# A hybrid conv and attention encoder layer on eight cores: attention moved one group further behind the projections, and the conv work regrouped

## The chip, the cores and the metric

The kernel runs on all 8 cores of one Trainium2 chip. Each core takes half of one prompt sequence (4,096 frames) and four sample streams, and no core waits for another. Times are device microseconds (us) of the slowest core. A ratio is the mean time of one kernel's fast runs over that of the other kernel's fast runs of the same rounds, so it is not quite the ratio of the medians that stand beside it.

Some executions fall in a slower state, in which one die or both show a lower granted TensorE clock. A variant is compared by its ratio to the kernel before on its own chip. For finer statements the cores of a die that the slow state left alone are used as well: in each run the slowest core of the less disturbed die, called the undisturbed die below. By that measure the kernel before takes 2670 to 2673 us (medians) on four chips. On the first chip it cannot be formed for the kernel before, whose runs there are on record without core clocks; its profiled run took 2678.91 us where the four timed runs took about 2700.

## The reference, cut to what matters

One encoder layer, applied to every frame:

```python
x = x + 0.5 * swiglu_ffn(x, g_ff1, w_ff1_in, w_ff1_out)            # first pass
z = rms_norm(x, g_mix) @ w_in                                      # the mixer starts here
cv, cg, q, k, v = jnp.split(z, SPLITS, axis=-1)
u = cv * jax.nn.sigmoid(cg)                                        # GLU, 512 channels
c_out = silu(layer_norm(depthwise_conv31(u_hist) + b_dw))
q = partial_rope(rms_norm(q, g_q), pos)                            # 8 heads of 64
k = partial_rope(rms_norm(k, g_k), pos)                            # 2 heads of 64
a_out = banded_window_attention(q, k, v, sinks)                    # own chunk of 64 and two before
x = x + jnp.concatenate([c_out, a_out], axis=-1) @ w_out           # the mixer ends here
x = x + 0.5 * swiglu_ffn(x, g_ff2, w_ff2_in, w_ff2_out)            # third pass
```

## The kernel before

The program has three passes: the first feed-forward pass (names that begin with A_), the mixer (B_) and the second feed-forward pass, here called the third pass (C_). The mixer handles 32 groups of 128 frames; eight groups make a conv tile. The Python code writes the operations in program order. From it come the dependencies. A list scheduler then assigns every operation a place in its engine's instruction stream, using assumed durations. Where an operation wasn't ready when its turn came, TensorE was seen to stand before it, for 3.27 us in the first timeline below. The names to know:

- B_xn, B_wi: projections (GLU, q, k, v). B_um: the GLU's result.
- B_qn: normed, rotated q and k. TensorE transposes it and VectorE copies the transpose to B_qkt, which the scores read.
- B_pt: the exponentials of the scores, B_ma: the attention result.
- B_us, B_wr: the conv's input and weights, B_y its output, B_yb a bf16 copy for the sums of the layer norm, B_lr the reciprocal deviation, B_z the conv's result.
- B_z goes through memory in another layout and comes back through the staging buffer B_mt into B_mc. The output projection multiplies B_mc and B_ma by B_wo and adds B_x.
- C_wu: weights of the third pass in 22 column groups. C_xb: its first normed blocks.

One step of the mixer, before:

```python
proj, att = n < NG, 1 <= n <= NG               # NG = 32 groups
...
if proj:
    self.glu_pe(n); self.glu_act(n)            # GLU projection, sigmoid
if att:
    self.transp(trq, 128, self.QKT[n % 4])     # transpose the q and k of the previous step
...
if cq is not None:
    self.conv_pe(cq[0], cq[1], 0)              # one pair of 32-channel conv groups a step, from step 10
    self.conv_pe(cq[0], cq[1], 1)
if att:
    self.scores(n - 1, 0)                      # scores that read the transpose made in this step
...
if att:
    self.scores(n - 1, 1)
tail_some(2)
if proj:
    self.qkv_pe(...)                           # q, k, v of group n
if att:
    self.pv(n - 1)
if proj:
    trq, f = self.qkv_post(n, ...)             # norm and rotation of q and k: ScalarE and VectorE
...                                            # from step 22: output projection of group n - 22
```

The conv of the first tile uses two accumulator banks, one of which the attention also uses:

```python
if t == 0:
    p = self.pb[6 if half == 0 else 4][:, 0:N]     # scores and pv use banks 4 and 5
else:
    p = self.pb[6][:, half * 256:half * 256 + 256]
```

Of the kernel before, what the change touches and what calls it, by code (L numbers as in the profile page):

```python
# [22 lines left out]
class _Op:  # L23
    __slots__ = ("eng", "fn", "idx", "lane", "seq", "deps", "raw", "waits", "know", "signal", "tok", "cost", "nbytes", "unit")


class Prog:
# [124 lines left out]
    def schedule(self, rounds=3):  # L152
# [15 lines left out]
        dma = [l[0].lane is not None for l in units]  # L168
        wire = [l[0].nbytes / 250e3 if d else 0.0 for l, d in zip(units, dma)]

# [55 lines left out]
        for i in range(rounds):  # L226
            start, order, t = run(preds, succs, prio, False)
            if best is None or t < best[0]:
                best = (t, order)
            start, _, _ = run(succs, preds, [-(start[u] + cost[u]) for u in range(n)], True)  # L230
            prio = [-(start[u] + cost[u]) for u in range(n)]
            self.trace.append(t)
        self.order = [o for u in best[1] for o in units[u]]
        self.model_us = best[0]

    def resolve(self):
# [97 lines left out]
class Ops:  # L334
# [4 lines left out]

    def cost(self, eng, meth, kw):  # L340
        out = kw.get("out", kw.get("ap"))
        n = free_size(kw["in_"] if meth == "tensor_reduce" else out)
        if eng == "tensor":
            if meth == "transpose":
                return 0.11 if kw["in_"].dtype == BF16 else 0.25
            return max(0.105, n / 2400.0 + 0.003)
        if eng == "scalar":
            ptr = sum(hasattr(kw.get(k), "tensor") for k in ("scale", "bias"))
            return 0.28 + 0.093 * max(0, ptr - 1) + n / 1200.0 + (0.2 if kw.get("accum_out") is not None else 0)
        if eng == "gpsimd":  # L350
            return 0.2 + n * 0.0022
        aps = [kw[k] for k in OUTS + INS if hasattr(kw.get(k), "tensor")]
        psum = any(self.P.info[a.tensor.name][0] == "p" for a in aps)
        one = meth in ("tensor_copy", "tensor_scalar")
        fast = 2.0 if one and not psum else 1.0
        if all(a.dtype == BF16 for a in aps) and meth in ("tensor_copy", "tensor_scalar", "tensor_tensor"):
            fast *= 2.0
        return 0.14 + n / 960.0 / min(fast, 4.0)

# [82 lines left out]
class FF:  # L442
# [3 lines left out]
    def __init__(self, K, carves, tag, wu, wd, g1, g2, blocks, src, dst, xnd=None, rkey=None, wkey=None, nkey=None, low=None, cwd=None, weng="gpsimd", hook=None):  # L446
# [14 lines left out]
        fits = NJ if low is None else (low - c1.off) // 4096  # L461
        self.WU = [(c1 if j < fits else c2)([128, 2048], BF16, "wu") for j in range(NJ)]
        c3 = c0 if cwd is None else cwd
# [195 lines left out]
GLAG = 22  # L659
NG = 32  # L660


class Mixer:
# [5 lines left out]
    def __init__(self, K, base):  # L669
# [18 lines left out]
        self.GE = [C([128, 512], F32, "ge") for _ in range(2)]  # L688
        self.UX = C([128, 4, 4, 56], BF16, "ux")
        self.VC = C([128, 4, 128], BF16, "vc")  # L690
        self.KCT = C([128, 4, 128], BF16, "kct")
        self.SMASK = C([64, 256], BF16, "smask")
        self.QKS = C([128, 5, 64], BF16, "qks")
        self.VS = C([64, 128], BF16, "vs")
        self.US32 = C([128, 4, 64], F32, "us32")
        self.U32 = self.US32[:, :, 0:32]
        self.QKT = [C([128, 5, 128], BF16, "qkt") for _ in range(4)]
        self.V = [C([128, 128], BF16, "v") for _ in range(4)]
        self.PT = [C([128, 2, 512], BF16, "pt") for _ in range(3)]
# [3 lines left out]
        self.WO = C([128, 8, 1024], BF16, "wo")  # L703
        self.MA = [C([128, 4, 128], BF16, "ma") for _ in range(GLAG - 1)]
        self.MC = C([128, 4, 1024], BF16, "mc")
# [11 lines left out]

        self.WR = [C([128, 2, 1152], BF16, "wr") for _ in range(2)]
        self.US_off = C.off
# [10 lines left out]
        self.LR = C([128, 304], F32, "lr")  # L730
        se = C.off
        self.SE = C([128, 4, 304], F32, "se")
        self.LT = self.SE[:, 3, :]
        self.OUT = P.sbuf("B_out", [128, 512], F32, se)
        self.Z = C([128, 4, 304], BF16, "z")
        self.ZS = C([128, 4, 16], BF16, "zs")
        self.ZT = C([128, 16, 16], BF16, "zt")
        self.MT = [P.sbuf("B_mt0", [128, 8, 256], BF16, se), P.sbuf("B_mt1", [128, 8, 256], BF16, y)]
        self.end = C.off
# [190 lines left out]
    def scores(self, G, kg):  # L930
        O = self.O
        two = self.two(2) if kg == 0 else self.two(4)
        K_ = self.QKT[(G + kg) % 4]
        Q = self.QKT[(G + 1) % 4]
        with self.O.group():
            for g in range(2):
                r = slice(g * 64, g * 64 + 64)
                O.mm(two[:, g * 512:(g + 1) * 512], K_[r, 4, :], Q[r, 0:4, :])
        pt = self.PT[self.nxt("pt", 3)]
        self.pts[kg] = pt  # L940
        O.act(out=pt[:, :, :].rearrange("p g n -> p (g n)"), in_=two, func=AF.Exp, scale=0.125)
# [4 lines left out]
    def pv(self, G):  # L946
# [3 lines left out]
        for half in range(2):  # L950
            ps = self.pb[4 + half]
            with self.O.group():
                combos = ((half, slice(0, 128)), (1 - half, slice(0, 64) if half == 0 else slice(64, 128)))
                for ci, (kg, rows) in enumerate(combos):
                    for what in range(2):
                        for g in range(2):
                            mv = self.pts[kg][rows, g, :].rearrange("p (j q) -> p j q", j=4)[:, :, half * 64:half * 64 + 64]
                            if what == 0:
                                w = self.V[(G + kg) % 4][rows, g * 64:(g + 1) * 64]
                            else:  # L960
                                w = self.ONE[rows, 1 if (G == 0 and kg == 0) else 0, :]
# [53 lines left out]
    def load_wd(self, q):  # L1015
        i = self.nxt("wr", 2)
        self.wr[q] = self.WR[i]
        self.O.dma("sync", "bwr%d" % i, self.WR[i][:, :, :], self.d.wdc[2 * q:2 * q + 2].rearrange("g p n -> p g n"),
                   rk=[("wdc", g, h) for g in (2 * q, 2 * q + 1) for h in range(2)])

    def conv_pe(self, t, q, half):
# [3 lines left out]
        if t == 0:  # L1025
            p = self.pb[6 if half == 0 else 4][:, 0:N]
        else:
# [4 lines left out]
        self.yps[half] = p  # L1032

    def conv_post(self, t, q):
        O = self.O
        N = 304 if t == 0 else 256
        sl = self.ypos % self.NY
        self.ypos += 2
        yb, y2 = self.YB[q % 2], self.Y2[q % 2]
        for h in range(2):  # L1040
            g = 2 * q + h
            O.act(out=self.Y[:, sl + h, 0:N], in_=self.yps[h], func=AF.Identity, bias=self.CP[:, 0, g:g + 1])
            self.yslot[(t, g)] = sl + h
        ys = self.Y[:, sl:sl + 2, 0:N]
# [126 lines left out]
    def run(self, on_step=None):  # L1171
# [3 lines left out]
        last_step = NG + GLAG  # L1175
        CL = 10

# [13 lines left out]
        def conv_at(n):  # L1191
            c = n - CL
            return divmod(c, 8) if 0 <= c < 32 else None

        trq = None
        for n in range(last_step):
            proj, att = n < NG, 1 <= n <= NG
            cq = conv_at(n)
            og = n - GLAG
            flush_late()  # L1200
            if n == 0:
# [4 lines left out]
                self.transp(QN, 128, self.QKT[0], q=False)  # L1206
            nq = conv_at(n + 1)
            if nq is not None:
                self.load_wd(nq[1])
            if 0 <= og + 1 < NG:  # L1210
# [5 lines left out]
            if proj:  # L1216
                self.glu_pe(n)
                self.glu_act(n)
            if att:
                self.transp(trq, 128, self.QKT[n % 4])  # L1220
            if self.stat:
                q = self.stat.pop()
                self.stats_pe(q[1])
                if q[1] == 7:
                    self.tails.append(self.tail(q[0]))
            if proj:
                self.glu_dve(n)
            if cq is not None:
                self.conv_pe(cq[0], cq[1], 0)
                self.conv_pe(cq[0], cq[1], 1)  # L1230
            if att:
                self.scores(n - 1, 0)
            if cq is not None:
                self.conv_post(cq[0], cq[1])
                self.stat.append((cq[0], cq[1]))
            if att:
                self.scores(n - 1, 1)
            tail_some(2)
# [5 lines left out]
            if att:  # L1244
                self.pv(n - 1)
            if proj:
                lastg = n == NG - 1
                trq, f = self.qkv_post(n, 128, self.two(2), self.V[(n + 1) % 4][:, :], k32=self.KO[:, :] if lastg else None,
                                       v32=self.VO[:, :] if lastg else None)
            if att:  # L1250
                self.late.append(self.softmax_group(n - 1))
            if proj:
                self.late.append(f)
            for h in range(2):
                tt = n - (6 + 2 * h) - (2 if h else 0)
                if tt >= 0 and tt % 8 == 0 and tt // 8 < 4:
                    self.load_us(tt // 8, h)
# [74 lines left out]
def build_nc():  # L1332
# [81 lines left out]
    def prologue():  # L1414
# [8 lines left out]
    c0 = Carve(P, base, "C")  # L1423
    c2 = Carve(P, M.US_off, "C_")
    Cc = FF(K, (c0, c0, c2), "C", d.wu2b, d.wd2b, d.gains[2], None, [main[0:2] + [samp]] + b3, d.x2, d.yout, rkey=lambda g: [("x2", g[0])],
            low=M.mid, weng="sync")
    assert c0.off <= M.US_off
    Cc.run(loads(Cc))
# [113 lines left out]
```

## Time and profile before

| | before |
|---|---|
| median of four runs | 2700.36 us (2697.87 to 2704.14) |
| span of the profiled core | 2677.2 us |
| TensorE busy over the span | 93% |

The mean of 93% hides where the time goes. This is the busy time by stretches of the kernel before, on its slowest core: from the end of the first pass to the first output projection, from there to the last group's projection, from there to the last output projection, and the third pass. Columns: the stretch, its length, then busy time (and number of instructions) of TensorE's matmuls, its weight loads, VectorE, ScalarE and GpSimd, then the granted TensorE clock, the busy share of the DMA engines, and GB/s.

```profile
1055.00:1401.00 346.00, 283.50 (x1817) 143.97 (x1815) 182.97 (x443) 191.36 (x324) 29.55 (x57) 0.88 0.30 78
1401.00:1534.00 133.00, 131.97 (x847) 70.45 (x846) 85.43 (x179) 77.22 (x132) 18.70 (x31) 0.99 0.56 168
1534.00:1740.00 206.00, 149.31 (x830) 79.80 (x828) 114.26 (x294) 75.88 (x112) 38.53 (x67) 0.85 0.70 224
1740.00:2677.00 937.00, 923.06 (x5351) 516.11 (x5349) 243.88 (x598) 162.71 (x304) 18.15 (x34) 0.99 0.17 58
```

Read the first row: TensorE idles for 346.0 - 283.5 = 62.5 us, and what it does it does at a mean clock of 0.88. In the second row it idles for 1 us: there the output projections give it something to do whatever else is late. In the third it idles for 57 us. No other engine is near its limit in the first row (VectorE 183 of 346 us), so it is waiting, not bandwidth, that costs time.

What TensorE waited for in that first stretch. Columns: who waited, for whom, the name of what it waited for, us in total, number of waits, the longest.

```profile
PE PS L363 <- DVE B_qn L363: 26.4, 9, 4.3
PE PS L363 <- DVE B_qkt L363: 8.1, 12, 1.0
PE PS L363 <- DVE B_t_95 L363: 6.0, 3, 2.9
PE PS L363 <- ACT B_y L363: 5.9, 1, 5.9
PE PS L363 <- DVE B_t_94 L363: 2.9, 1, 2.9
```

More than half of it is the chain of one group's q and k: norm on ScalarE and VectorE (B_qn), transpose on TensorE, copy on VectorE (B_qkt), scores on TensorE. The timeline of TensorE in the kernel before shows one such place (start, us, engine, operation, operands, and in brackets the idle time just before and its releaser):

```profile
1270.82 0.27 PE L363 MATMUL PS<-B_y_170,B_e_158 128*128 128x256 bf16 x1
1274.37 0.44 PE L363 MATMUL PS<-K_t,B_qn 128*128 128x128 bf16 x5 [3.27 <-DVE B_qn L363]
1275.08 2.44 PE L363 MATMUL PS<-B_us,B_wr 128*128 128x304 bf16 x9 [0.27 <-DVE B_ma L363]
```

TensorE stands for 3.27 us before the five transposes (B_qn). The nine conv matmuls after the gap take 2.44 us; the same nine take 1.33 us elsewhere in this trace. The granted clock over those 2.44 us was 0.50. The gap is paid twice, once as idle time and once as slow matmuls. The slow ones need not be the first: after the gap of 2.93 us that ends at 1287.26 us the nine took 1.35 us, and the next nine, at 1290.86, took 2.46 us.

After the last projection, TensorE of the kernel before waited for:

```profile
PE PS L363 <- DVE C_xb L363: 19.8, 2, 10.6
PE PS L363 <- DVE B_mc_164 L363: 9.9, 2, 5.9
PE PS L363 <- DMA B_wr<-wdc: 6.4, 1, 6.4
PE PS L363 <- DMA C_wu<-wu2b: 5.0, 1, 5.0
```

### The profile page before, as it was taken

Reading aid. Unit: us, or ns where it says so; the run is one execution under the profiler, and the core shown is the slowest. Engines: PE = TensorE matmul, PEld = TensorE weight load, DVE = VectorE, ACT = ScalarE, POOL = GpSimd, SP = SyncE. Lnnn points to the kernel's source line nnn. Section 1 sums busy time; section 2 is a strip of 40 time slices with the busy share of each in tenths; the row PEclk is TensorE's granted clock in tenths of the full one; section 3 lists DMA queues with packets and bytes.
Section 4 is the critical chain, followed back from the end, with each engine's and each line's share of the span. In section 5 each row is a group of like instructions: output and inputs, shape, how many; then the busy total and the mean of one; then the engine's idle time right before and its main releaser. Section 6 shows DMA issues by size and latency. Waiting matters only on the chain.

```text
span 2677.2 us, 41546 instructions; the slowest of 8 cores (2662.2 to 2677.2 us)
## 1 busy us (share of the span) xinstructions
PE 2485.1 (93%) x14740; PEld 1367.4 (51%) x14740; DVE 1030.0 (38%) x2717; ACT 764.4 (29%) x1311; POOL 224.7 (8%) x398
## 2 busy tenths in 40 slices
PE   1999999999999999798869976799999999999998
PEld 1555555555555555344435543355555555555554
DVE  2253344334433424444467556422232333223211
ACT  1222232223222312555466545011111121112110
POOL 2010111011100001000021111200000000000000
PEclk9999999999999999898879988899999999999999
DMA  9943444345433344122235685750121112110110
GB/s 196 173 124 79 87 116 107 80 96 120 119 80 85 87 124 143 36 57 79 71 97 151 207 266 171 228 191 29 48 71 48 42 54 72 56 48 32 48 48 24
DMA packets 113698, 266.93 MB, mean 100 GB/s; under 512 B 33631, under 2 KB 51039, under 8 KB 112535
## 3 DMA queue, kind: packets, MB, share of 16 engines
q0 software_dynamic: 36416, 131.81, 19.5%
q1 hardware_dynamic: 77079, 132.46, 17.2%
q8 instruction: 121, 1.98, 0.3%
q14 instruction: 82, 0.67, 0.1%
HBM read 230.89 MB, written 97.86 MB: 123 GB/s over the span
## 4 chain that ended last, share of the span: by engine, by line
PE 85%; DMA 7%; DVE 4%; issue 2%; ACT 1%; DVEq 0%; POOL 0%; ACTq 0%; POOLq 0%; SPq 0%
PE PS L363 85%; DMA A_wd<-wd 4%; DVE B_y L363 1%; DMA B_wr<-wdc 1%; DMA xnt<-A_xo 0%; DMA A_wu<-wu 0%; DMA B_x_152<-x 0%; DVE B_qs L363 0%; DVE C_sm L363 0%; DMA C_xa<-x 0%; ACT B_sq L363 0%; DVE B_t_94 L363 0%; DVE B_qn L363 0%; ACT B_se L363 0%; DMA x<-B_x_152 0%
## 5 line engine op out<-in xcount | busy, mean ns | idle before, releaser
L363 PE MATMUL PS<-A_xnt,A_wu 128*128 128x384 bf16 (+1 forms) x3872 | 651.0, 329 | 1.8 <-ACT A_xnt L363 1.0
L363 PE MATMUL PS<-C_xnt,C_wu 128*128 128x384 bf16 (+1 forms) x3872 | 628.0, 324 | 6.3 <-DMA C_wu<-wu2b 5.0
L363 PEld LDWEIGHTS PS<-A_xnt,A_wu 128*128 128x128 bf16 x3872 | 377.3, 98 | 258.9 <-issue 6.4
L363 PEld LDWEIGHTS PS<-C_xnt,C_wu 128*128 128x128 bf16 x3872 | 378.4, 98 | 247.1 <-issue 6.9
L363 ACT ACTIVATE C_sa<-PS 128x384 f32<-128x384 f32 (+1 forms) x242 | 117.5, 486 | 757.7 <-PE PS L363 724.7
L363 PE MATMUL PS<-A_wd,A_h 128*128 128x512 bf16 (+1 forms) x1496 | 327.1, 379 | 2.4 <-DMA A_wd<-wd 2.4
L363 PE MATMUL PS<-C_wd,C_h 128*128 128x512 bf16 (+1 forms) x1452 | 315.3, 379 | 0.0
L363 DVE TENSOR_TENSOR C_h<-PS,C_sa 128x384 bf16<-128x384 f32 (+1 forms) x242 | 133.3, 551 | 368.6 <-PE PS L363 362.0
L363 DVE TENSOR_TENSOR A_h<-PS,A_sa 128x384 bf16<-128x384 f32 (+1 forms) x242 | 136.2, 563 | 330.5 <-PE PS L363 329.0
L363 ACT ACTIVATE A_sa<-PS 128x384 f32<-128x384 f32 (+1 forms) x242 | 120.1, 496 | 411.4 <-PE PS L363 376.2
L363 PEld LDWEIGHTS PS<-A_wd,A_h 128*128 128x128 bf16 (+1 forms) x1496 | 146.3, 98 | 175.3 <-issue 3.8
L363 PEld LDWEIGHTS PS<-C_wd,C_h 128*128 128x128 bf16 (+1 forms) x1452 | 142.7, 98 | 169.5 <-issue 0.4
L363 DVE SCALAR_TENSOR_TENSOR C_xr<-PS,C_xr 128x512 f32<-128x512 f32 (+1 forms) x66 | 45.6, 691 | 270.6 <-PE PS L363 270.6
L363 PE MATMUL PS<-B_xn,B_wi 128*128 128x512 bf16 x512 | 123.6, 390 | 2.1 <-ACT B_ge L363 0.9
L363 ACT ACTIVATE A_xb<-A_xr 128x1024 bf16<-128x1024 f32 (+1 forms) x34 | 36.0, 1057 | 285.5 <-DVE A_xr L363 266.8
L363 DVE SCALAR_TENSOR_TENSOR A_xr<-PS,A_xr 128x512 f32<-128x512 f32 (+1 forms) x68 | 46.8, 689 | 160.2 <-PE PS L363 160.2
L363 PE MATMUL PS<-B_us,B_wr 128*128 128x256 bf16 (+1 forms) x576 | 91.6, 315 | 17.3 <-DMA B_wr<-wdc 6.4
L363 PE MATMUL PS<-B_wi,B_xn 128*128 128x256 bf16 (+1 forms) x512 | 94.1, 338 | 0.8 <-ACT B_pt L363 0.8
L407 POOL DMA_DIRECT2D yout<-C_xr x33 | 17.6, 534 | 909.3 <-DVE C_xr L363 909.3
L363 PE MATMUL PS<-K_t,A_xb 128*128 128x128 bf16 (+1 forms) x544 | 42.0, 223 | 53.5 <-DVE A_sm L363 31.3
L363 PEld LDWEIGHTS PS<-B_us,B_wr 128*128 128x128 bf16 x576 | 60.2, 109 | 46.6 <-issue 27.2
L363 PEld LDWEIGHTS PS<-B_xn,B_wi 128*128 128x128 bf16 x512 | 48.5, 100 | 61.8 <-issue 15.1
(169 smaller groups left out, 2033.2 us busy)
## 6 DMA issues: line engine op xcount, KB each, us to landing
B_wr<-wdc SPq DMA_DIRECT2D x32, 576.0 KB, 4.8
A_xa<-xin SPq DMA_DIRECT2D x33, 512.0 KB, 5.4
A_xr<-xin SPq DMA_DIRECT2D x33, 512.0 KB, 3.7
x<-A_xr POOLq DMA_DIRECT2D x33, 512.0 KB, 2.9
C_xa<-x SPq DMA_DIRECT2D x32, 512.0 KB, 3.7
C_xr<-x SPq DMA_DIRECT2D x32, 512.0 KB, 3.7
yout<-C_xr POOLq DMA_DIRECT2D x32, 512.0 KB, 2.9
A_wu<-wu POOLq DMA_DIRECT2D x22, 512.0 KB, 39.0
```

The source lines that it names most:

```text
L363: o = self.P.add(eng, lambda e: getattr(e, meth)(**kw), r, w, cost=self.cost(eng, meth, kw))
L407: self.P.add(eng, lambda e: e.dma_start(out=out, in_=in_), r, w, lane=lane, rk=rk, wk=wk, cost=1.0 if eng == "gpsimd" else 0.5, nbytes=n * ...
```

## The change

The intent: give the chain of one group's q and k a whole step more before its result is needed; do a tile's conv in four steps and leave the next four free of conv, so that its layer norm on VectorE can spread over eight; put the first tile's conv in one bank; load the third pass's weights so that those whose memory comes free last are used last; and correct the scheduler's assumed durations. Its core, with cuts:

```diff
# scheduler: assumed durations (cut)
-        wire = [l[0].nbytes / 250e3 ...]
+        wire = [l[0].nbytes / (210e3 if l[0].eng == "gpsimd" else 290e3) ...]
-        fast = 2.0 if one and not psum else 1.0          # assumed of VectorE: single-source operations twice as fast
+        if meth == "tensor_copy":                        # assumed of copies alone
+            fast = (2.0 if half else 1.0) if psum else (4.0 if half else 2.0)
# buffers
-        self.QKT = [... for _ in range(4)]; self.V = [... for _ in range(4)]
+        self.QKT = [... for _ in range(5)]; self.V = [... for _ in range(5)]
-        self.OUT = P.sbuf("B_out", [128, 512], F32, se)              # shared with the norm's scratch
+        self.OUT = self.GE[0]
-        self.MT = [P.sbuf("B_mt0", [128, 8, 256], BF16, se), ...]    # shared with the norm's scratch
+        self.MT = [C([128, 8, 256], BF16, "mt"), ...]
# mixer step
-            proj, att = n < NG, 1 <= n <= NG
+            proj, tra, att = n < NG, 1 <= n <= NG, 2 <= n <= NG + 1
-                self.scores(n - 1, 0) ... self.scores(n - 1, 1) ... self.pv(n - 1)
+                self.scores(n - 2, 0) ... self.scores(n - 2, 1) ... self.pv(n - 2)
-        CL = 10
-            c = n - CL
-            return divmod(c, 8) if 0 <= c < 32 else None
+        CL = 8
+            t, r = divmod(n - CL, 8)
+            return [(t, 2 * r), (t, 2 * r + 1)] if 0 <= t < 4 and r < 4 else []
-            p = self.pb[6 if half == 0 else 4][:, 0:N]
+            p = self.pb[6][:, 0:N]                 # tile 0: evict the first half before the second
+                self.load_wd((q + 2) % 8)          # conv weights two pairs ahead
# third pass's weights
-        self.WU = [(c1 if j < fits else c2)([128, 2048], BF16, "wu") for j in range(NJ)]
+        self.WU = [c1([128, 2048], BF16, "wu") for j in range(min(fits, NJ))]
+        self.WU += [c2([128, 2048], BF16, "wu") for j in range(fits, NJ)][::-1]
```

More of the change, by code (lines that the diff above doesn't have):

```diff
@@ L23 @@
 class _Op:
-    __slots__ = ("eng", "fn", "idx", "lane", "seq", "deps", "raw", "waits", "know", "signal", "tok", "cost", "nbytes", "unit")
+    __slots__ = ("eng", "fn", "idx", "lane", "seq", "deps", "raw", "waits", "know", "signal", "tok", "cost", "nbytes", "unit", "t")
 class Prog:
@@ L168, in schedule @@
         dma = [l[0].lane is not None for l in units]
-        wire = [l[0].nbytes / 250e3 if d else 0.0 for l, d in zip(units, dma)]
+        wire = [l[0].nbytes / (210e3 if l[0].eng == "gpsimd" else 290e3) if d else 0.0 for l, d in zip(units, dma)]
         def run(before, after, prio, back):
@@ L228, in schedule @@
             if best is None or t < best[0]:
-                best = (t, order)
+                best = (t, order, start)
             start, _, _ = run(succs, preds, [-(start[u] + cost[u]) for u in range(n)], True)
@@ L234, in schedule @@
         self.model_us = best[0]
+        for u, l in enumerate(units):
+            for o in l:
+                o.t = best[2][u]
     def resolve(self):
@@ L344, in cost @@
             if meth == "transpose":
-                return 0.11 if kw["in_"].dtype == BF16 else 0.25
-            return max(0.105, n / 2400.0 + 0.003)
+                return 0.1 if kw["in_"].dtype == BF16 else 0.25
+            w = kw["lhsT"].ap
+            t = n / 2400.0 + 0.005
+            if w[0][1] <= 64 and w[-1][1] > 64:
+                return 0.75 * t
+            if w[-1][1] <= 64:
+                return max(0.06, 0.78 * t)
+            return max(0.101, t)
         if eng == "scalar":
             ptr = sum(hasattr(kw.get(k), "tensor") for k in ("scale", "bias"))
-            return 0.28 + 0.093 * max(0, ptr - 1) + n / 1200.0 + (0.2 if kw.get("accum_out") is not None else 0)
+            return 0.2 + 0.093 * ptr + n / 1200.0 + (0.2 if kw.get("accum_out") is not None else 0)
         if eng == "gpsimd":
@@ L353, in cost @@
         psum = any(self.P.info[a.tensor.name][0] == "p" for a in aps)
-        one = meth in ("tensor_copy", "tensor_scalar")
-        fast = 2.0 if one and not psum else 1.0
-        if all(a.dtype == BF16 for a in aps) and meth in ("tensor_copy", "tensor_scalar", "tensor_tensor"):
-            fast *= 2.0
-        return 0.14 + n / 960.0 / min(fast, 4.0)
+        half = all(a.dtype == BF16 for a in aps)
+        fast = 1.0
+        if meth == "tensor_copy":
+            fast = (2.0 if half else 1.0) if psum else (4.0 if half else 2.0)
+        return 0.15 + n / 960.0 / fast
     def op(self, eng, meth, **kw):
@@ L660 @@
 NG = 32
+NWR = 2
 class Mixer:
@@ L688, in __init__ @@
         self.GE = [C([128, 512], F32, "ge") for _ in range(2)]
-        self.UX = C([128, 4, 4, 56], BF16, "ux")
-        self.VC = C([128, 4, 128], BF16, "vc")
-        self.KCT = C([128, 4, 128], BF16, "kct")
-        self.SMASK = C([64, 256], BF16, "smask")
-        self.QKS = C([128, 5, 64], BF16, "qks")
-        self.VS = C([64, 128], BF16, "vs")
         self.US32 = C([128, 4, 64], F32, "us32")
         self.U32 = self.US32[:, :, 0:32]
-        self.QKT = [C([128, 5, 128], BF16, "qkt") for _ in range(4)]
-        self.V = [C([128, 128], BF16, "v") for _ in range(4)]
+        self.QKT = [C([128, 5, 128], BF16, "qkt") for _ in range(5)]
+        self.V = [C([128, 128], BF16, "v") for _ in range(5)]
         self.PT = [C([128, 2, 512], BF16, "pt") for _ in range(3)]
@@ L703, in __init__ @@
         self.WO = C([128, 8, 1024], BF16, "wo")
-        self.MA = [C([128, 4, 128], BF16, "ma") for _ in range(GLAG - 1)]
+        ma = C.off
+        self.MA = [C([128, 4, 128], BF16, "ma") for _ in range(GLAG - 2)]
+        S = Carve(P, ma + 12 * 1024, "S")
+        self.UX = S([128, 4, 4, 56], BF16, "ux")
+        self.VC = S([128, 4, 128], BF16, "vc")
+        self.KCT = S([128, 4, 128], BF16, "kct")
+        self.SMASK = S([64, 256], BF16, "smask")
+        self.QKS = S([128, 5, 64], BF16, "qks")
+        self.VS = S([64, 128], BF16, "vs")
+        assert S.off <= C.off
         self.MC = C([128, 4, 1024], BF16, "mc")
@@ L716, in __init__ @@
         self.KS, self.VSO = self.KO, self.VO
-        self.WR = [C([128, 2, 1152], BF16, "wr") for _ in range(2)]
+        self.high = C.off
+        self.WR = [C([128, 2, 1152], BF16, "wr") for _ in range(NWR)]
         self.US_off = C.off
@@ L730, in __init__ @@
         self.LR = C([128, 304], F32, "lr")
-        se = C.off
         self.SE = C([128, 4, 304], F32, "se")
         self.LT = self.SE[:, 3, :]
-        self.OUT = P.sbuf("B_out", [128, 512], F32, se)
+        self.OUT = self.GE[0]
         self.Z = C([128, 4, 304], BF16, "z")
@@ L737, in __init__ @@
         self.ZT = C([128, 16, 16], BF16, "zt")
-        self.MT = [P.sbuf("B_mt0", [128, 8, 256], BF16, se), P.sbuf("B_mt1", [128, 8, 256], BF16, y)]
+        self.MT = [C([128, 8, 256], BF16, "mt"), P.sbuf("B_mt1", [128, 8, 256], BF16, y)]
         self.end = C.off
@@ L932, in scores @@
         two = self.two(2) if kg == 0 else self.two(4)
-        K_ = self.QKT[(G + kg) % 4]
-        Q = self.QKT[(G + 1) % 4]
+        K_ = self.QKT[(G + kg) % 5]
+        Q = self.QKT[(G + 1) % 5]
         with self.O.group():
@@ L958, in pv @@
                             if what == 0:
-                                w = self.V[(G + kg) % 4][rows, g * 64:(g + 1) * 64]
+                                w = self.V[(G + kg) % 5][rows, g * 64:(g + 1) * 64]
                             else:
@@ L1015, in load_wd @@
     def load_wd(self, q):
-        i = self.nxt("wr", 2)
+        i = self.nxt("wr", NWR)
         self.wr[q] = self.WR[i]
@@ L1032, in conv_pe, with conv_out @@
         self.yps[half] = p
+    def conv_out(self, t, q, h):
+        N = 304 if t == 0 else 256
+        g = 2 * q + h
+        sl = self.ypos % self.NY
+        self.ypos += 1
+        self.O.act(out=self.Y[:, sl, 0:N], in_=self.yps[h], func=AF.Identity, bias=self.CP[:, 0, g:g + 1])
+        self.yslot[(t, g)] = sl
     def conv_post(self, t, q):
@@ L1036, in conv_post @@
         N = 304 if t == 0 else 256
-        sl = self.ypos % self.NY
-        self.ypos += 2
+        sl = self.yslot[(t, 2 * q)]
         yb, y2 = self.YB[q % 2], self.Y2[q % 2]
-        for h in range(2):
-            g = 2 * q + h
-            O.act(out=self.Y[:, sl + h, 0:N], in_=self.yps[h], func=AF.Identity, bias=self.CP[:, 0, g:g + 1])
-            self.yslot[(t, g)] = sl + h
         ys = self.Y[:, sl:sl + 2, 0:N]
@@ L1206, in run @@
                 self.transp(QN, 128, self.QKT[0], q=False)
-            nq = conv_at(n + 1)
-            if nq is not None:
-                self.load_wd(nq[1])
+            if n == CL - 1:
+                self.load_wd(0)
+                self.load_wd(1)
             if 0 <= og + 1 < NG:
@@ L1218, in run @@
                 self.glu_act(n)
-            if att:
-                self.transp(trq, 128, self.QKT[n % 4])
-            if self.stat:
-                q = self.stat.pop()
+            if tra:
+                self.transp(trq, 128, self.QKT[n % 5])
+            for q in self.stat:
                 self.stats_pe(q[1])
@@ L1225, in run, with conv @@
                     self.tails.append(self.tail(q[0]))
+            self.stat = []
             if proj:
                 self.glu_dve(n)
-            if cq is not None:
-                self.conv_pe(cq[0], cq[1], 0)
-                self.conv_pe(cq[0], cq[1], 1)
+            def conv(t, q):
+                for h in range(2):
+                    self.conv_pe(t, q, h)
+                    if t == 0:
+                        self.conv_out(t, q, h)
+                if t > 0:
+                    for h in range(2):
+                        self.conv_out(t, q, h)
+                if t < 3 or q < 6:
+                    self.load_wd((q + 2) % 8)
+                self.conv_post(t, q)
+                self.stat.append((t, q))
+            if cq:
+                conv(*cq[0])
             if att:
-                self.scores(n - 1, 0)
-            if cq is not None:
-                self.conv_post(cq[0], cq[1])
-                self.stat.append((cq[0], cq[1]))
+                self.scores(n - 2, 0)
+            if cq:
+                conv(*cq[1])
             if att:
-                self.scores(n - 1, 1)
+                self.scores(n - 2, 1)
             tail_some(2)
@@ L1244, in run @@
             if att:
-                self.pv(n - 1)
+                self.pv(n - 2)
             if proj:
                 lastg = n == NG - 1
-                trq, f = self.qkv_post(n, 128, self.two(2), self.V[(n + 1) % 4][:, :], k32=self.KO[:, :] if lastg else None,
+                trq, f = self.qkv_post(n, 128, self.two(2), self.V[(n + 1) % 5][:, :], k32=self.KO[:, :] if lastg else None,
                                        v32=self.VO[:, :] if lastg else None)
             if att:
-                self.late.append(self.softmax_group(n - 1))
+                self.late.append(self.softmax_group(n - 2))
             if proj:
@@ L1254, in run @@
             for h in range(2):
-                tt = n - (6 + 2 * h) - (2 if h else 0)
+                tt = n - (6 + 2 * h)
                 if tt >= 0 and tt % 8 == 0 and tt // 8 < 4:
@@ L1423, in build_nc @@
     c0 = Carve(P, base, "C")
-    c2 = Carve(P, M.US_off, "C_")
+    c2 = Carve(P, M.high, "C_")
     Cc = FF(K, (c0, c0, c2), "C", d.wu2b, d.wd2b, d.gains[2], None, [main[0:2] + [samp]] + b3, d.x2, d.yout, rkey=lambda g: [("x2", g[0])],
             low=M.mid, weng="sync")
-    assert c0.off <= M.US_off
+    assert c0.off <= M.high
     Cc.run(loads(Cc))
```

## The prediction

> **What bounds the kernel.** TensorE is 93% busy of a 2677 us span (page), but the table by stretches splits it. First feed-forward pass (to about 1055 us) and third (from 1745 us) run TensorE without gaps at granted clock 1.00, apart from the weight-load start of about 55 us. The mixer between loses time (TensorE busy, clock): 1070 to 1200 us 110 of 130, 0.89; 1200 to 1400 us 159 of 200, 0.86; 1400 to 1540 us 139 of 140, 0.98; 1540 to 1745 us 144 of 205, 0.85. That is some 124 us idle, and the half-clock stretches after each gap cost perhaps 30 to 50 more (estimate: one minus clock, times busy time). A nine-matmul conv group took 2.44 us after a 2.9 us gap and 1.33 us otherwise[...]. No other engine limits: VectorE 372 and ScalarE 335 us of 675.
>
> **Where TensorE waits** (list of waits, timeline). To 1400 us: on the normed q (B_qn) 26 us in nine waits, on its transposed copy (B_qkt) 8 us in twelve, on the chain around tile 0's second conv half 9 us in three (it shares a bank with the attention output), 5.9 us once while the first tile's layer norm holds VectorE at 10 of 10 us (1340 to 1360). After 1540 us: 16 us of the chain is a conv-weight load landing late among the third pass's weights, 20 us in two waits for C_xb, 10 us for the last conv tile's return (B_mc), 13 us on x buffers, 5 us for C_wu.
>
> **What the change does.** No work is added or removed. (1) Attention one group later: scores no longer follow the transpose of the same step; removes most B_qkt waits and lets other work cover part of the B_qn ones. (2) Conv in four steps per tile, two pairs a step, then four without; bank sharing with attention goes, at the price of a wait for the 0.5 us eviction between tile 0's halves. Tile 3's conv and norm end about six steps sooner, so the last eight output projections should be ready sooner; conv weights are fetched two pairs ahead. (3) The norm's VectorE work (about 23 us a tile, from 0.68 us operations) is spread, its scratch no longer shared with the reload. (4) Third pass's blocked weights come last: about sixteen instead of eleven of the first block's column groups (2.1 us each) can fill gaps. (5) Scheduler costs now match traced durations (scalar-pointer operation of 256: 0.41 us against 0.27 assumed).
>
> **Sum.** To 1400 us: 20 to 45 us. 1400 to 1540: nothing. After 1540: 20 to 60 us. Middle: 70 us, all on the critical path.
>
> Predicted 2630 us, 8 in 10 between 2580 and 2685. Chances: faster by over 2% 0.66, within 2% 0.31, slower 0.03.
>
> **Signs.** Right: waits on B_qn plus B_qkt under half; clock above 0.92 between mixer start and the first output projection; no 16 us conv-weight wait; the C_wu wait gone; third pass's uninterrupted run begins 50 to 90 us sooner. Wrong: new waits on B_y evictions (bank 6), on B_us loads, or on XN; or the mixer's end unchanged.
>
> **What would break it.** Every instruction's place is recomputed: steps without conv may lack filler and starve; or the last tile's round trip through memory still sets the end.

## The result

| | before | after |
|---|---|---|
| median of four runs | 2700.36 us | 2628.21 us (two slow runs among them; of the four fast ones 2625.0) |
| fast runs | 2697.87 to 2704.14 us | 2613.08 to 2630.18 us |
| ratio of the fast runs | | 0.9714, 95% interval 0.9678 to 0.9749 |
| span of the profiled core | 2677.2 us | 2611.4 us |
| mean granted clock over the cores | 0.970 to 0.974 | 0.979 to 0.987 |

The same four stretches of the kernel after, on its slowest core, cut at the same events:

```profile
1055.00:1336.00 281.00, 261.79 (x1781) 138.03 (x1778) 170.82 (x407) 176.61 (x311) 28.07 (x56) 0.94 0.39 99
1336.00:1478.00 142.00, 140.56 (x903) 73.19 (x902) 102.80 (x217) 87.57 (x148) 18.11 (x31) 0.99 0.49 148
1478.00:1676.00 198.00, 155.43 (x912) 85.14 (x911) 109.34 (x287) 67.50 (x106) 38.73 (x67) 0.87 0.73 232
1676.00:2611.00 935.00, 912.80 (x5256) 507.46 (x5254) 241.21 (x592) 158.91 (x298) 18.16 (x34) 0.99 0.18 58
```

The lengths went from 346, 133, 206, 937 to 281, 142, 198, 935 us: 65 us less before the first output projection, 9 more in the second stretch (which now holds more work, for example 217 VectorE instructions instead of 179), 8 less at the mixer's end, 2 less in the third pass. The sum is 66 us, the difference of the two spans. In the first stretch TensorE's idle time fell from 62.5 to 281.0 - 261.8 = 19.2 us and its clock rose from 0.88 to 0.94.

What TensorE waits for in the first stretch of the kernel after, the first three lines:

```profile
PE PS L373 <- ACT B_pt L373: 6.7, 9, 1.5
PE PS L373 <- DVE B_lr L373: 2.6, 1, 2.6
PE PS L373 <- DVE B_qkt L373: 2.3, 3, 1.6
```

B_qn is gone from this list and B_qkt fell from 8.1 to 2.3 us. The timeline of TensorE in the kernel after shows the new order, in which a late B_qn need not stop it:

```profile
1207.42 0.39 PE L373 MATMUL PS<-B_qkt 64*128 64x512 bf16 x2
...
1210.34 1.89 PE L373 MATMUL PS<-B_wi,B_xn 128*128 128x512 bf16 x8
...
1212.99 0.44 PE L373 MATMUL PS<-K_t,B_qn 128*128 128x128 bf16 x5
...
1215.13 0.43 PE L373 MATMUL PS<-B_qkt 64*128 64x512 bf16 x2
```

Between the projection of q, k and v at 1210.34 and the scores at 1215.13 stand the transposes of an earlier group, and none of these lines has an idle time in brackets. VectorE had finished the B_qn that they read 2.3 us earlier (its last operation ran from 1209.84 us for 0.82 us). By the program, the scores read transposes that were made a step ago.

After the last projection TensorE of the kernel after waits for other things, but hardly less (56 us in all, where the kernel before has 62):

```profile
PE PS L373 <- DMA B_wr<-wdc: 18.6, 2, 14.2
PE PS L373 <- DVE B_x_153 L373: 11.0, 2, 9.0
PE PS L373 <- DMA C_wu<-wu2b: 7.6, 1, 7.6
```

The conv weights (B_wr) cost more than before: 18.6 us against 6.4. The queue of SyncE in the kernel after shows what was put in before them (start, us, operands, count):

```profile
1512.07 1.65 SPq L417 DMA_DIRECT2D C_wu<-wu2b  x3
1513.78 0.66 SPq L417 DMA_DIRECT2D C_xa<-x  x1
1514.49 0.49 SPq L417 DMA_DIRECT2D C_wu<-wu2b  x1
...
1516.04 3.35 SPq L417 DMA_DIRECT2D C_wu<-wu2b  x3
1520.76 4.51 SPq L417 DMA_DIRECT2D B_wr<-wdc  x2
```

And the chain of work that ended last, in the kernel after, passes through the load issued at 1520.76, which took 25.50 us to land; the median of these loads is 4.9 us:

```profile
1520.76 25.50 DMA B_wr<-wdc
```

The conv weights of the last tile and the third pass's weights go through one queue, and within the 11 us before, seven loads of the latter (512 KB each) and two blocks of the third pass's input (C_xa) had been put in, over 4 MB together. In what order the queue's loads were served, no view here shows. Nor was the queue alone: from 1520 to 1546 us the DMA engines were busy almost throughout, at 336 GB/s, and GpSimd's queue moved 3.76 of the 8.74 MB. How much of the delay each gave wasn't separated.

### The profile page after: what moved, and what is told of

It is laid out like the page before. It is cut to its first block, busy times and chain, and to the rows that moved or that the text cites. A ratio compares the mean times of both kernels' runs of the same rounds, so it can differ in the third digit from the quotient of the medians.

```text
span 2611.4 us, 41531 instructions; the slowest of 8 cores (2584.0 to 2611.4 us)
## 1 busy us (share of the span) xinstructions
PE 2468.5 (95%) x14740; PEld 1361.1 (52%) x14740; DVE 1030.4 (39%) x2717; ACT 745.6 (29%) x1303; POOL 223.8 (9%) x398
## 4 chain that ended last, share of the span: by engine, by line
PE 91%; DMA 4%; DVE 1%; ACT 1%; issue 1%; SPq 0%; DVEq 0%; POOL 0%; ACTq 0%; POOLq 0%
PE PS L373 91%; DMA B_wr<-wdc 2%; DMA A_xa<-xin 1%; DMA A_g_51<-gains 0%; ACT B_pt L373 0%; DMA B_x_153<-x 0%; DMA C_wu<-wu2b 0%; ACT B_se L373 0%; DVE A_sm L373 0%; ACT B_ge L373 0%; DVE A_xb L373 0%; DVE C_sm L373 0%; DMA x<-B_x_152 0%; DVE B_y L373 0%; SPq L417 0%
## 5 line engine op out<-in xcount | busy, mean ns | idle before, releaser
L373 PE MATMUL PS<-B_wi,B_xn 128*128 128x256 bf16 (+1 forms) x512 | 101.4, 351 | 4.3 <-ACT B_pt L373 4.3
L373 PE MATMUL PS<-B_us,B_wr 128*128 128x256 bf16 (+1 forms) x576 | 80.9, 290 | 20.4 <-DMA B_wr<-wdc 18.6
L373 DVE SCALAR_TENSOR_TENSOR A_sm<-A_sm 128x1 f32<-128x1 f32 (+1 forms) x408 | 64.4, 159 | 35.5 <-DVE A_sm L373 1.5
```

The lines of the kernel that those rows point to most:

```text
L373: o = self.P.add(eng, lambda e: getattr(e, meth)(**kw), r, w, cost=self.cost(eng, meth, kw))
```

## The experiments

Twelve runs were made (ten new kernels, and the changed kernel twice more), all with correct results. Several take the change apart; two try to mend the mixer's end. Because the scheduler recomputes every place after any edit, an edit moves instructions that it doesn't name. Two measures are used beside the ratio: TensorE's waits, and the time from 1055 us (where the mixer starts in all of them) to the last group's projection and from there to the last output projection, read from the slowest core's trace (the last digit can be one off).

| run | what it is | ratio to before (95%) | to last projection | then to last output projection |
|---|---|---|---|---|
| before | | 1 | 479 us | 206 us |
| after, first chip | all of the change | 0.9714 (0.9678 to 0.9749) | 423 | 198 |
| a_again | the same, second chip | 0.9757 (0.9741 to 0.9773) | 422 | 194 |
| a_ref | the same, third chip | 0.9760 (0.9720 to 0.9799) | 419 | 199 |
| u_att | after, attention one behind | 0.9870 (0.9855 to 0.9886) | 453 | 201 |
| u_conv | after, conv in eight steps | 0.9787 (0.9720 to 0.9854) | 434 | 182 |
| u_cost | after, old scheduler costs | 0.9709 (0.9688 to 0.9730) | 418 | 192 |
| u_wu | after, old weight order | 0.9714 (0.9698 to 0.9729) | 413 | 192 |
| d_att | before, attention two behind | 0.9791 (0.9771 to 0.9810) | 427 | 194 |
| d_conv | before, conv part alone | 0.9870 (0.9758 to 0.9982) | 437 (a core of the undisturbed die) | 188 |
| d_bank | before, tile 0 in one bank | one fast run: 2672.61 against 2671.93 to 2675.95 us | 477 | 199 |
| d_cost | before, new scheduler costs | 1.0018 (0.9998 to 1.0038) | 485 | 198 |
| f_late | after, third-pass weights held | 0.9743 (0.9723 to 0.9762) | 417 | 194 |
| f_late_mt | f_late and a second staging buffer | 0.9680 (0.9666 to 0.9695) | 407 | 193 |

### a_again and a_ref: the changed kernel on other chips

No edit.

> The changed kernel itself, so that the variants can be compared with it on one chip. Ratio to the kernel before 0.971, give or take 0.003.

> The changed kernel again, on the chip of the two runs that follow: 0.971 to 0.976 of the kernel before.

They gave 0.9757, outside the expected 0.971 give or take 0.003, and 0.9760, at the edge of what was expected. The gain is there on three chips, between 2.4 and 2.9%. The kernel before took about 1% longer on the first chip than on the others, so the 2.4% are the better guide; on the undisturbed dies the changed kernel takes 2601 to 2604 us (medians) on all three. It was not run in the rounds of the four variants that begin with u_.

### u_att: the change without the attention's distance

```diff
-            proj, tra, att = n < NG, 1 <= n <= NG, 2 <= n <= NG + 1
+            proj, tra, att = n < NG, 1 <= n <= NG, 1 <= n <= NG
-    scores(n - 2, ..), pv(n - 2), softmax_group(n - 2)
+    scores(n - 1, ..), pv(n - 1), softmax_group(n - 1)      # and one more buffer for the attention results
```

> The changed kernel with attention put back one group behind the projections, everything else kept. Theory A (the extra group of distance is what freed the front of the mixer): TensorE's waits on B_qn and B_qkt before the last projection, 3.6 us in the changed kernel, come back to over 20 us, and the time returns to 2660 to 2690 us. Rival (the conv arrangement or the scheduler's costs did it): waits on B_qn and B_qkt stay under 12 us and the time stays within 15 us of the changed kernel's, near 2625.

The ratio was 0.9870 (all four runs 2639.66 to 2644.63 us, kernel before about 2678 on this chip). The waits of TensorE in its first stretch:

```profile
PE PS L373 <- DVE B_qn L373: 12.8, 9, 4.1
PE PS L373 <- DVE B_qkt L373: 7.7, 9, 1.9
```

Together 20.5 us, where the changed kernel has 2.3 and the kernel before 34.5: theory A stands on the waits. The 2640 to 2645 us as measured miss its 2660 to 2690, but these were written for a kernel before of 2700 us; 0.9870 of 2700 is 2665, inside that range. The same holds for the absolute times expected of u_conv, u_cost and u_wu. But the rest of the change is worth 1.3% without it.

### d_att: the kernel before with the attention's distance alone

```diff
-    QKT, V: 4 buffers;  scores(n - 1, ..), pv(n - 1), softmax_group(n - 1)
+    QKT, V: 5 buffers;  scores(n - 2, ..), pv(n - 2), softmax_group(n - 2)
```

> The kernel before with attention two groups behind and nothing else (the sample's mask moved over the attention results to make room). Theory A, the distance suffices by itself: ratio 0.980 to 0.986, the waits on B_qn and B_qkt before the last projection from 35 us down to under 8 us. Rival, it needs the conv's rearrangement with it (tile 0's second conv half still shares a bank with the attention output): ratio 0.990 or more.

The ratio was 0.9791, on the chip on which the whole change gave 0.9757. It rests on two fast runs (2616.55 and 2618.38 us), since four of six were slow; but the undisturbed dies of all six runs, 2612 to 2618 us against 2668 to 2672, agree. One step of distance gives 2.1 of 2.4%. The stretches to the first output projection and to the last projection show it (same columns as above):

```profile
1055.00:1350.00 295.00, 267.40 (x1818) 140.19 (x1815) 182.11 (x442) 184.65 (x321) 30.12 (x58) 0.92 0.35 91
1350.00:1482.00 132.00, 132.00 (x868) 69.82 (x867) 86.12 (x182) 79.45 (x135) 18.85 (x32) 1.00 0.60 177
```

and the waits of the first stretch:

```profile
PE PS L363 <- DVE B_ma L363: 9.3, 2, 6.0
...
PE PS L363 <- DVE B_qkt L363: 2.2, 3, 1.5
...
PE PS L363 <- DVE B_qn L363: 0.9, 2, 0.6
```

B_qn and B_qkt fell from 34.5 to 3.1 us, and 52 of the 56 us that the whole change saves up to the last projection are saved here too (479 to 427, against 423). The rival, that the conv's rearrangement is needed with it, falls.

### d_conv: the conv part alone

This is u_att with the old scheduler costs and the old weight order put back as well: conv in four steps, tile 0 in one bank, conv weights two pairs ahead, separate scratch, a fifth buffer for the transposed q and k.

> The conv part alone: the changed kernel with attention one group behind, the old scheduler costs and the old order of the third pass's weights (what is left of the change: conv in four steps, tile 0's bank, conv weights two pairs ahead, separate scratch, a fifth buffer for transposed q and k). The run that undid only the attention's distance gave 0.987; if the conv part is what remained there, this gives 0.985 to 0.990. If costs and weight order mattered together with it, 0.993 or more.

The ratio was 0.987: two fast runs (2647.48 and 2651.02 us) against three of the kernel before (2675.74, 2677.89 and 2698.74), hence the wide interval. Both fast runs have two cores at a clock of 0.97, so the undisturbed dies tell more: 2626 to 2630 us in five of the six runs, against 2668 to 2674 in all seven of the kernel before, a ratio of 0.984. u_att has 0.987 by the same measure. So the conv part by itself is worth about 1.6%, and 1.3% when the new costs and weight order go with it (u_att). The two parts don't add up: 2.1% and 1.6% singly, 2.4% together on the chip where the first and the sum were both measured. Both cut the same waits: on a core of the undisturbed die of d_conv, B_qn and B_qkt come to 18.4 us in the whole mixer, where the kernel before has 34.9.

### u_conv: the change with the conv in eight steps

```diff
-        CL = 8;   t, r = divmod(n - CL, 8); two pairs a step in four of eight steps
+        CL = 10;  one pair in each step, as before     # and the second load of the conv's input two steps later, as before
```

> The changed kernel with one conv pair a step in eight steps, starting at step 10 as before; banks, buffers, attention distance and scheduler costs kept. Theory B (the conv in four steps pays): 2650 to 2680 us, with the first output projection as late as before. Rival (its value is only the bank and the earlier data, which are kept): within 15 us of 2625.

It gave 0.9787, with runs at 2607, 2607 and 2633 us in the fast state. The two that agree are within 10 us of the variants u_cost and u_wu on the same chip (2598 to 2602), and on the undisturbed dies the four runs give 2605 to 2608 us, where the changed kernel has medians of 2601 to 2604 in its own rounds. So the four-step form is worth a few tenths of a per cent at most once attention has its distance, far from what theory B expected. The first output projection came at 1338 us, not late, against theory B.

### u_cost and d_cost: the scheduler's costs

> The changed kernel scheduled with the old costs of operations and of DMA. Theory C (the corrected costs are a real part of the gain): 10 to 40 us slower than the changed kernel, with more waits of TensorE on VectorE results in the mixer. Rival (the structure pays, the costs are near enough): within 10 us of 2625.

> The kernel before, scheduled with the new costs and nothing else. Theory: without the attention's distance the rest of the change still gave 1.3 per cent; if the corrected costs are that rest, the ratio is near 0.987. If the conv's arrangement is, the ratio is 0.997 to 1.003.

With the old costs the changed kernel has 0.9709, with the new ones the kernel before has 1.0018. The corrected durations, though right (a 128x256 operation with per-partition scalars takes 0.41 us in the trace where 0.27 had been assumed), gave nothing by themselves in either kernel. One thing in u_cost is worth a look, together with u_wu, in which only the weight order is undone. TensorE's waits for the conv weights, first in u_cost, then in u_wu:

```profile
PE PS L366 <- DMA B_wr<-wdc: 3.2, 1, 3.2
PE PS L373 <- DMA B_wr<-wdc: 5.1, 1, 5.1
```

The changed kernel has 16.3 to 18.9 us of them on three chips, and u_att and u_conv, which have the new costs and the new order as well, 15.7 and 12.8. With either of the two undone the long wait is gone (d_conv, with both undone, has 3.3 after its last projection). The loads show a difference: the slowest load of conv weights took 25.5 us to land in the changed kernel and 16.3 in u_wu. During the 20 us before its last two the changed kernel put in seven loads of third-pass weights.

### u_wu: the third pass's weights in the old order

```diff
-        self.WU += [c2(...) for j in range(fits, NJ)][::-1]
+        self.WU = [(c1 if j < fits else c2)(...) for j in range(NJ)]
```

> The changed kernel with the third pass's column groups laid out in ascending order again, so that those on the last freed memory come in the middle of the first block. If the order is worth what was forecast: fewer column groups run before the mixer's last output projection (ten instead of sixteen), the time rises by 5 to 15 us to about 2635. If the tail is bound by something else, the time stays within 5 us of 2625.

The ratio was 0.9714, that of the full change on the first chip and no worse than on any other; the changed kernel wasn't run in these rounds. The mechanism works: counted in the traces, 17 column groups (272 matmuls of 16 each) had run in the changed kernel when the last output projection ran, 12 (192) in u_wu, 11 (176) in the kernel before. It pays nothing that these runs show. The likely reason, not tested by itself, is that the groups that are done early are not what the last output projection waits for.

### d_bank: tile 0's conv in one bank, in the kernel before

```diff
-            p = self.pb[6 if half == 0 else 4][:, 0:N]
+            p = self.pb[6][:, 0:N]      # and evict the first half before the second
```

> The kernel before with tile 0's conv halves both in bank 6, each evicted before the next, and nothing else. If the shared bank cost what the waits say (9 us in three waits and the half clock after them): ratio 0.993 to 0.997. If the wait only moves to the eviction or to the next q: 0.998 to 1.002.

Three of its four runs fell in the slow state, so there is no interval; the one fast run, 2672.61 us, lies within the fast runs of the kernel before, and the undisturbed dies of all four, 2666 to 2671 us against 2668 to 2672, agree: nothing gained, as expected if the wait only moves. Its waits in the first stretch show where the 9 us went:

```profile
PE PS L363 <- DVE B_qn L363: 21.4, 7, 4.3
PE PS L363 <- DVE B_yb L363: 10.8, 5, 2.2
PE PS L363 <- DVE B_qkt L363: 8.7, 12, 1.4
```

The waits on B_t, behind the shared bank, are gone (in the kernel before, three of them, of 2.92, 2.93 and 2.93 us, had each been followed within 6 us by nine matmuls that took 2.44 to 2.46 us), and 10.8 us on B_yb have come in their place. The wait moved, though not to the eviction (B_y), which has 5.9 us as before. The first stretch took 343 us instead of 346.

### f_late: hold the third pass's weights back

```diff
     def load_wd(self, q, last=False):
-        ... rk=[...])
+        ... rk=[...], wk=[("wrl",)] if last else [])     # the mixer's last conv weights
-        k = [("pc", self.tag + "u", j)] ...
+        k = [("pc", self.tag + "u", j), ("wrl",)] ...     # third-pass column groups wait for them
```

> The changed kernel with the third pass's column-group weights held until the mixer's last conv weights have landed. Theory D (5 MB of third-pass weights crowd out the last conv weights; TensorE waits 18.6 us on B_wr in the changed kernel): waits on B_wr under 4 us and the ratio 0.005 to 0.008 under the changed kernel's. Rival (the mixer's end is bound by the last tile's norm and its round trip through memory, or the weights then come too late): waits move to B_mc, B_x or C_wu and the ratio stays within 0.003.

The ratio was 0.9743 against 0.9757 on the same chip, and the intervals overlap; theory D wanted 0.005 to 0.008 less. Waits of f_late after the last projection:

```profile
PE PS L373 <- DVE C_xb L373: 15.5, 1, 15.5
PE PS L373 <- DVE C_sm L373: 8.5, 4, 5.6
...
PE PS L373 <- DMA B_wr<-wdc: 5.7, 2, 3.3
```

The wait for conv weights fell from 18.6 to 5.7 us, and TensorE stood 15.5 us before a transpose of the third pass (C_xb) instead, which ran ahead of output projections (at 1555.20 us, the next of these at 1569.03). The late weights are a real wait, but not the limit of the mixer's end.

### f_late_mt: and a second staging buffer

```diff
-        self.MT = [C(...), P.sbuf("B_mt1", [128, 8, 256], BF16, y)]
+        self.MT = [C(...), P.sbuf("B_mt1", [128, 8, 256], BF16, xe)]   # memory that is free by then
-            st = self.MT[r if t == 3 else 0]
+            st = self.MT[r]                                           # each half its own buffer
```

> The changed kernel with the third pass's weights held as in the run that delayed them, and a second staging buffer (on memory that is free by then) for the second half of each conv tile's return, so that its load need not wait for the first half's copy. If the return of the third tile's second half is what the mixer's end waits for: 8 to 15 us under the changed kernel, TensorE's waits after the last projection under 30 us. If the last tile's norm and the x buffers bind, within 5 us of it.

Its fast runs took 2586.72 to 2591.07 us, those of the changed kernel on that chip 2601.41 to 2632.80. The ratios are 0.9680 and 0.9760 and their intervals don't overlap: this version beats both kernels, the changed one by 0.8% (0.7% on the undisturbed dies, medians of 2582 and 2602 us). The expected mechanism isn't what the trace shows, though. Of the 19 us between the two profiled spans (2608.1 and 2589.4), 12 lie before the last projection and 6 after it, and the waits after it still add up to 49 us, where under 30 had been expected:

```profile
PE PS L373 <- DVE B_x L373: 18.7, 7, 5.4
PE PS L373 <- DVE B_mc L373: 6.4, 1, 6.4
```

Whether the buffer itself or the schedule that came out with it gave the first 12 us wasn't tested; nor was the second buffer run without the held weights.

## Why the prediction was right, and where its sum was wrong

The predicted time, 2630 us, met the measured 2628 (2625 without the slow runs), and faster by over 2% came true. Point by point:

- **TensorE's waiting bounds the mixer, and the gaps cost twice.** Right. In the first stretch the idle time fell by 62.5 - 19.2 = 43 us. One minus clock, times busy time, fell from 0.12 x 283.5 = 34 us to 0.06 x 261.8 = 16 us, an estimate of another 18 us. Together 61 of the 65 us that this stretch lost. The same nine matmuls took 2.44 us after gaps of 2.92 and 3.27 us and 1.33 us without one; over the 2.44 us after the gap of 3.27 us the granted clock was 0.50.
- **Attention one group later.** The mechanism was right, and the size was too small. The waits on B_qn and B_qkt fell from 34.5 us in this stretch to 2.3. The prediction spoke of "part of the B_qn" waits; d_att shows that nearly all of them go, with nothing else changed, and that this alone is worth 2.1%.
- **"To 1400 us: 20 to 45 us."** Too small: the time to the first output projection fell by 65 us and the time to the last projection by 56. The reason is the point before (d_att alone saves 52 of the 56), and the clock that rose with it.
- **"After 1540: 20 to 60 us."** The term of the sum that was mis-sized: it measured 8 us to the last output projection, and 2 more in the third pass. The steps of the prediction under it were that the last tile's conv and norm would end earlier and that conv weights fetched two pairs ahead would not be late. Both failed. Counted from the last projection, the last conv matmul began after 78 us where the kernel before had 69; it came 47 us sooner only because the last projection came 56 us sooner. The conv weights cost 18.6 us of waits instead of 6.4; their last loads were put into one queue after the third pass's weights, and u_cost and u_wu show that it took the new costs and the new weight order together. f_late then showed that removing this wait uncovers the next.
- **The bank.** The prediction put 9 us of waits down to it and gave no separate size to the "price" it named, a wait for an eviction. In the kernel before, d_bank found nothing gained: 10.8 us of new waits came, on B_yb and not on the eviction. The first stretch of the changed kernel has no wait on B_yb in its list.
- **The corrected scheduler costs** were listed without a size; they gave nothing (u_cost, d_cost).
- **The weight order.** The mechanism was right to the number (about sixteen groups forecast, 17 counted), but "the C_wu wait gone" was wrong: the wait is 7.6 us where it was 5.0, and the trace shows three of the groups loaded only at 1676.09 us, when the last output projection's matmuls were under way. u_wu shows no gain from it.
- **Signs.** Waits on B_qn plus B_qkt under half: right. Clock above 0.92 before the first output projection: right, 0.94. The third pass's uninterrupted run 50 to 90 us sooner: it begins at 1684 instead of 1746 us, with one more break of 5.6 us. No long conv-weight wait: wrong. Of the signs against it, no new waits on B_y, B_us or XN are in the list of the first stretch, but "the mixer's end unchanged" came close to true (206 to 198 us). The feared starving of steps without conv did not come to more than single waits (2.6 us on B_lr, 6.7 us in nine waits on B_pt).

So the total was right partly by luck: against the middles of the two ranges, one term was about 20 us too small (56 against 32) and the other some 30 us too large (10 against 40).

What stays open: how much of u_conv's small difference is the four-step form and how much the schedule; what sets the mixer's end, where each wait removed uncovered another; and why f_late_mt gains before the last projection.

## What to carry to other kernels

Where one engine waits for a short chain on other engines in every step, let the consumer lag one more step and pay the buffers (here 1.5 KB a partition for q, k and v): it costs no work and was worth 2.1%. Several remedies for the same idle time don't add up, so test each alone before adding another. And when a pass's bulk weights share a queue with loads that the pass before still needs, look in the trace at how much is put in before them (here over 4 MB, and 25.5 us to land); but look at what waits next before counting on the gain.

## What the runs show of the granted clock

- In the profiles of the kernel before and the kernel after, TensorE of the slowest core was busy for all 800 us from 200 to 1000 us, at a granted clock of 1.00; the stretch from 1676 to 2611 us of the kernel after has 0.99. In the slow state the mean clock of a core went down to 0.81: in one run of d_conv cores 0 to 3 had 0.806 to 0.813 and spans of 3074 to 3096 us, cores 4 to 7 had 0.981 to 0.985 and 2617 to 2630 us. In another both dies were lower, at 0.818 to 0.825 and at 0.929 to 0.938.
- The mean clock was lower where TensorE waited about 3 us in many steps for the chain through ScalarE and VectorE: 0.88 over 346 us with nine waits on B_qn, 26.4 us, in the kernel before, and 0.92 over 295 us in d_att, where 0.9 us of these waits are left.
